# Three equal column groups in the first projection, x staged in a slab, six held-back K tiles and a norm shift on TensorE, in a hybrid encoder block

## The chip, the cores and the metric

The kernel runs on one core of a Trainium2 chip. The metric is the device time of one execution in microseconds (us). Before the change it is 1144.58 us, the median of three runs (1144.49 to 1145.9).

The engines are TensorE (PE; its loads of stationary operands are PEld), VectorE (DVE), ScalarE (ACT), GpSimd (POOL) and SyncE (SP). In this kernel SP issues nearly all loads and stores.

## The reference

One layer, 256 tokens, width 2048, float32. A combined input projection feeds eight retention heads and eight latent-attention heads; both groups are joined by an output projection. Then a norm, a feed-forward part and a second norm:

```
proj = x @ w_in                       # retention q, k, v, gate | latent c_q (768), c_kv (512), k_rope (64)
mix  = concat(retention(...), latent_attention(...)) @ w_out
x    = LN(alpha * x + mix, ln1_g, ln1_b)
h    = square(relu(x @ w_up)) @ w_down        # 2048 -> 8192 -> 2048
out  = LN(alpha * x + h, ln2_g, ln2_b)
```

with `LN(x) = (x - mean) * rsqrt(var + eps) * g + b` over the 2048 features. The 1344 latent columns of the input projection (c_q, c_kv and k_rope) and the second LN are what the change touches.

## The kernel before

**Exact products in two halves.** Each float32 operand is split into a high part, which TensorE can multiply in its faster float32r form, and a low part, the rest. ACT writes the high part (`nc.scalar.copy`, L166), DVE subtracts it from the original for the low part (L167). A product is three TensorE products: high by high, high by low, low by high. `xstat` (L264 to L277) issues them with the activations as the stationary operand and the weights moving, for each K tile, each block of 128 tokens (`tb` 0 and 1), and each group of columns. It takes a list of steps (K tiles) and, for a single bank of results, the number of that bank. `wstat` does the same with the weights stationary.

**The stream of loads.** All weights are jobs in one list, in the order of their use. A job has a load (one DMA on SP into one of `NRAW` = 3 raw buffers of 128x2048, L147 to L152) and pieces of work (`piece`, up to 1024 columns each) that split it into a high and a low tile. These tiles come from `NSLOT` = 5 slots (`wsp`); jobs with `into` are staged into other memory and take no slot. `unit()` stands between products and issues up to two further pieces, if a slot is free by the order of the program; `use(job)` issues whatever is still missing. `load_ahead` (L108) issues the loads of the job in hand and the two behind it. A load into a raw buffer waits until ACT and DVE have split what was in it. The engines run their own instructions strictly in the order in which the program issued them, so a split that waits for its load holds up what stands behind it on ACT and DVE.

**Head.** The activations x come transposed, in five loads (`x_job`, L197; after weights 0, 1, 3, 6 and 10 by `X_AFTER`). Each takes a raw buffer of the same three, and DVE splits it into `xhl`. The first weight tile is loaded in four DMAs (columns 0, 256, 512, 1024 to 1343) and split in as many steps. Meanwhile eight TensorE products on zeros (L351) are issued. Then come 16 K tiles of the latent columns (L365 to L377): for each block of tokens nine products, three parts by groups of 512, 512 and 320 columns (`MW`, L353), into six banks of PSUM. A slab `ml` of 128x8192 later holds the latent values. Slabs are three large buffers used in turn. The results are copied into it (L373) and the retention projection starts (`r` in the profile).

**Middle.** Retention, latent attention, output projection, first norm and the up product follow; the change leaves them alone.

**End.** The down product has 64 K tiles (L881), each 24 products into all eight banks (two blocks of tokens by four groups of 512 columns). The activations of four K tiles at a time are split by `r_split` (L853: ACT L857, DVE L858), issued ahead, where kt is 1, 5, 9 and so on. K tiles 60 to 63 are held back: 60 and 61 are staged in a slab (`wst2`), 62 and 63 sit in slots. They are then multiplied bank after bank (`down_bank`, L900), 12 products a bank, so that DVE can add the residual and take statistics (`residual`, L655) of one bank while TensorE works on the next. After the last bank of a block `stats` (L686) gives mean and variance, with a power on POOL (L250) for the reciprocal root. The norm is then applied in place. `finish` (L909) makes two updates on DVE and a store on SP; `finish_aside` (L918) has ACT normalise, POOL multiply by the gain and add the shift, and ACT's queue store. The first block's columns 0 to 1023 go through `finish` between the second block's banks, its columns 1024 to 2047 aside; of the second block 1536 to 2047 go aside and the rest to `finish`.

Of the kernel before, what the change touches and what calls it, by code (L numbers as in the profile page):

```python
# [33 lines left out]
NRAW = 3  # L34
NSLOT = 5
# [3 lines left out]
class Cols:  # L39
    """Columns held in pieces of 1024."""  # L40

    def __init__(self, pieces):
        self.pieces = pieces

    def __getitem__(self, key):
        i, a = divmod(key[1].start, 1024)
        return self.pieces[i][:, a:a + key[1].stop - key[1].start]


class Job:  # L50
    """One load and the pieces of work that it feeds."""

    def __init__(self, load, pieces, slotted):
        self.load = load
        self.pieces = pieces
        self.slotted = slotted
        self.emitted = 0
        self.hi = []
        self.lo = []
        self.raw = None  # L60


@with_exitstack
def kernel(
# [43 lines left out]
    def load_ahead(upto):  # L108
        while state["dma"] < min(upto, len(jobs)):
            jobs[state["dma"]].load()  # L110
            state["dma"] += 1

    def next_piece(force):
# [9 lines left out]
        load_ahead(state["job"] + NRAW)  # L123
# [4 lines left out]
    def use(job, n=None):  # L128
        while job.emitted < (len(job.pieces) if n is None else n):
            next_piece(True)  # L130
        return Cols(job.hi), Cols(job.lo)
# [10 lines left out]
    def weights(src, n, name, first=False, into=None):  # L142
        job = Job(None, [], into is None)
        cuts = [0, 256, 512, 1024, n]

        def load():
            raw = raw_tile(job, f"raw_{name}")  # L147
            if first:
                for a, b in zip(cuts, cuts[1:]):
                    nc.sync.dma_start(raw[:, a:b], src[:, a:b])  # L150
            else:
                nc.sync.dma_start(raw[:, :n], src)  # L152

        def piece(i):
            a, m = i * 1024, min(1024, n - i * 1024)
# [7 lines left out]
            for o, e in ((0, 256), (256, 512), (512, 1024)) if first and i == 0 else ((0, m),):  # L163
                c = slice(o, e)
                r = job.raw[:, a + c.start:a + c.stop]
                nc.scalar.copy(hi[:, c], r)  # L166
                nc.vector.tensor_sub(lo[:, c], r, hi[:, c].bitcast(F32))  # L167

        job.load = load
        job.pieces = [lambda i=i: piece(i) for i in range((n + 1023) // 1024)]  # L170
# [11 lines left out]
    # side streams advance one stage for each unit of the main stream of products  # L182
# [12 lines left out]
    xhl = slab.tile([P, KT, 512], F32R, tag="slab", name="xhl")  # L195

    def x_job(k0, n):  # L197
        def load(job):
            nc.sync.dma_start(raw_tile(job, f"xraw{k0}")[:, : n * S], x_t[:, k0 * S:(k0 + n) * S])

        def piece():
            v = job.raw[:, : n * S].rearrange("p (k t) -> p k t", k=n)
# [3 lines left out]
        job = other(load, [piece])  # L206

# [44 lines left out]
    def rot(dst1, dst2, raw, cs, sn, n, w):  # L252
        """Rotate n pairs of halves, all first halves ahead of all second ones; raw is used up."""
# [86 lines left out]
    for kt in range(64):  # L340
        j_down.append(weights(w_down[kt], 2048, f"wd{kt}", into=staged_down(kt - 60) if kt in (60, 61) else None))
# [689 lines left out]
```

## Time and profile before

The profile is of one execution; its times are in us from the start.

| | |
|---|---|
| runs | 1144.58 us median (1144.49, 1144.58, 1145.9) |
| profiled execution's span | 1144.0 us |
| TensorE busy | 1127.5 us |
| VectorE, ScalarE, GpSimd busy | 687.6, 506.7, 18.2 us |
| HBM read, written | 214.12 MB, 2.10 MB |
| first product of the latent columns | 4.97 |
| first product of the retention projection | 68.30 |
| first held-back product | 1109.96 |
| residual of the last bank on VectorE starts | 1131.92 |

In the rows that follow, a group of instructions is written as line, engine, operation, result<-operands, shape and count (x16). A row of the timeline or of the chain begins with its start and how long it took; several like instructions in a row are merged, and the brackets give the engine's idle time before the first of them and what ended it. A row of a table by stretches has, after the stretch, its length, the busy time of PE, PEld, DVE, ACT and POOL with counts, TensorE's granted clock (1.00 is full), the busy share of the DMA engines and GB/s. A row of DMA issues ends with the size of one and the median time from issue to landing. Products overlap in TensorE's pipeline, so what one of them costs is the distance between starts and not the duration shown for one.

### The profile page before, as it was taken

The numbers are of one execution on the slowest core, as the hardware profiler recorded it, in microseconds if no ns is written. First come the engines' busy times: TensorE is split into PE (matmuls) and PEld (weight loads), VectorE is DVE, ScalarE is ACT, GpSimd is POOL, SyncE is SP. The second block draws the span as 40 slices with busy tenths as digits, with TensorE's granted clock in tenths as the row PEclk, the third lists the DMA queues.
The fourth block names the chain that finished last, engine by engine and source line by source line (L and its number), as shares of the span: only waits on it lengthen the run. The fifth ranks groups of instructions, "written<-read, shape, count | busy, mean of one in ns | idle before, by whom it ended". The sixth has DMA issues, their size and how long they took to land.

```text
span 1144.0 us, 14163 instructions
## 1 busy us (share of the span) xinstructions
PE 1127.5 (99%) x5636; PEld 952.7 (83%) x5636; DVE 687.6 (60%) x919; ACT 506.7 (44%) x653; POOL 18.2 (2%) x23
## 2 busy tenths in 40 slices
PE   8999999999999999999999999999999999999995
PEld 7888888888888889888888888888888888888884
DVE  5776674666656786555555655555656455445567
ACT  4445664545453545444444444444434444344340
POOL 0000000000000000000000000000000000000003
PEclk9999999999999999999999999999999999999998
DMA  7765364444474625555555555555566555555561
GB/s 227 254 210 208 116 222 178 157 148 160 152 294 177 236 103 196 190 188 190 189 188 185 185 184 184 184 185 184 187 223 237 199 184 189 203 197 184 189 252 74
DMA packets 34049, 217.12 MB, mean 190 GB/s; under 512 B 4160, under 2 KB 5312, under 8 KB 10560
## 3 DMA queue, kind: packets, MB, share of 16 engines
q1 hardware_dynamic: 33552, 215.44, 53.2%
q8 instruction: 44, 0.72, 0.2%
q10 hardware_dynamic: 432, 0.79, 0.2%
q14 instruction: 21, 0.17, 0.0%
HBM read 214.12 MB, written 2.10 MB: 189 GB/s over the span
## 4 chain that ended last, share of the span: by engine, by line
PE 95%; DVE 2%; DMA 1%; POOL 1%; ACT 1%; issue 0%; SPq 0%; ACTq 0%; DVEq 0%; POOLq 0%
PE d L274 29%; PE up L584 20%; PE r L274 15%; PE up L585 10%; PE o L274 7%; PE m L274 4%; PE pu L584 2%; DMA raw_mla<-in_w_mla 1%; PE pv L274 1%; PE pu L585 1%; PE pq L274 1%; PE up L746 1%; PE pms L608 0%; PE pms L607 0%; PE up L754 0%
## 5 line engine op out<-in xcount | busy, mean ns | idle before, releaser
L584 PE MATMUL up<-x1hl,hi_wu 128*128 128x512 f32 x984 | 347.7, 399 | 0.0
L585 PE MATMUL up<-x1hl,lo_wu 128*128 128x256 f32 x984 | 276.4, 281 | 0.0
L274 PE MATMUL d<-hi_wd,rhl 128*128 128x512 f32 x992 | 248.4, 389 | 0.0
L167 DVE TENSOR_TENSOR lo_wd<-raw_wd,hi_wd 128x1024 fp32r<-128x1024 f32 x124 | 146.6, 1221 | 158.3 <-ACT hi_wd L166 158.1
L584 PEld LDWEIGHTS up<-x1hl,hi_wu 128*128 128x128 f32 x984 | 184.9, 188 | 46.0
L274 PEld LDWEIGHTS d<-hi_wd,rhl 128*128 128x128 f32 x992 | 186.2, 188 | 38.6
L166 ACT CAST hi_wd<-raw_wd 128x1024 fp32r<-128x1024 f32 x124 | 125.1, 1053 | 191.3 <-PE d L274 182.8
L167 DVE TENSOR_TENSOR lo_wu<-raw_wu,hi_wu 128x1024 fp32r<-128x1024 f32 x128 | 156.4, 1225 | 74.1 <-ACT hi_wu L166 70.0
L585 PEld LDWEIGHTS up<-x1hl,lo_wu 128*128 128x128 f32 x984 | 185.9, 189 | 0.0
L166 ACT CAST hi_wu<-raw_wu 128x1024 fp32r<-128x1024 f32 x128 | 134.1, 1051 | 83.0 <-PE up L584 80.7
L274 PE MATMUL r<-hi_ret,xhl 128*128 128x512 f32 x512 | 147.1, 397 | 0.0
L274 PE MATMUL d<-lo_wd,rhl 128*128 128x512 f32 x496 | 134.5, 389 | 0.0
L274 PEld LDWEIGHTS d<-lo_wd,rhl 128*128 128x128 f32 x496 | 93.1, 188 | 19.3
L274 PEld LDWEIGHTS r<-hi_ret,xhl 128*128 128x128 f32 x512 | 93.9, 188 | 18.3
L167 DVE TENSOR_TENSOR lo_ret<-raw_ret,hi_ret 128x1024 fp32r<-128x1024 f32 x64 | 75.7, 1220 | 23.0 <-ACT hi_ret L166 22.9
L274 PE MATMUL r<-lo_ret,xhl 128*128 128x512 f32 x256 | 79.4, 391 | 0.0
L847 ACT COPY ut<-up 128x256 f32<-128x256 f32 x64 | 23.9, 373 | 118.9 <-PE up L585 116.2
L166 ACT CAST hi_ret<-raw_ret 128x1024 fp32r<-128x1024 f32 x64 | 64.9, 1051 | 14.5 <-PE r L274 11.6
L848 DVE TENSOR_TENSOR ut<-ut,up 128x256 f32<-128x256 f32 x64 | 27.0, 421 | 65.3 <-ACT ut L847 65.3
L274 PE MATMUL o<-hi_wo,mix 128*128 128x512 f32 x208 | 57.1, 392 | 0.0
L274 PEld LDWEIGHTS r<-lo_ret,xhl 128*128 128x128 f32 x256 | 48.0, 188 | 10.4
L274 PE MATMUL m<-hi_mla,xhl 128*128 128x512 f32 (+1 forms) x192 | 46.1, 372 | 0.9 <-ACT hi_mla L166 0.8
(182 smaller groups left out, 980.7 us busy)
## 6 DMA issues: line engine op xcount, KB each, us to landing
raw_wu<-in_w_up SPq DMA_DIRECT2D x64, 1024.0 KB, 4.8
raw_wd<-in_w_down SPq DMA_DIRECT2D x64, 1024.0 KB, 4.8
raw_ret<-in_w_ret SPq DMA_DIRECT2D x32, 1024.0 KB, 4.8
raw_wo<-in_w_out SPq DMA_DIRECT2D x16, 1024.0 KB, 4.8
raw_mla<-in_w_mla SPq DMA_DIRECT2D x15, 672.0 KB, 5.5
raw_qk<-in_w_qk SPq DMA_DIRECT2D x8, 640.0 KB, 3.9
row<-in_ln_rows SPq DMA_DIRECT2D x4, 1024.0 KB, 4.8
raw_uv<-in_w_uv SPq DMA_DIRECT2D x2, 1024.0 KB, 4.7
```

What stands on the lines that cost most here:

```text
L166: nc.scalar.copy(hi[:, c], r)
L167: nc.vector.tensor_sub(lo[:, c], r, hi[:, c].bitcast(F32))
L274: nc.tensor.matmul(accs[j][:, :w], x_part, w_part[:, a:a + w], start=first and fst and i == 0, stop=last and lst and i == len(steps) - 1)
L584: nc.tensor.matmul(pb, hi[:, a:a + P], hl[:, k0 + i], start=first and i == ks[0], stop=False)
L585: nc.tensor.matmul(pb[:, 0:S], lo[:, a:a + P], hl[:, k0 + i, 0:S], start=False, stop=last and i == ks[-1])
L746: nc.tensor.matmul(pb[:, :, t], hi[:, k * P:(k + 1) * P], x1hl[:, k].rearrange("p (a t) -> p a t", a=2)[:, :, t], start=tb == 0 and k == 0 ...
L847: nc.scalar.copy(t, pb[:, S:])
L848: nc.vector.tensor_add(t, t, pb[:, 0:S])
```

## The change

1. **Columns.** The latent columns are taken in three groups of 448 (`MW`), and their weight pieces are 896 and 448 columns wide rather than 1024 and 320 (`width`).
2. **x.** The x loads go to the front of the slab `ml`, which is allocated earlier and is empty at that time, and no longer take raw buffers (`raw_user`). `load_ahead` counts raw buffers only: three weight loads ahead, and every x load that stands before the next one.
3. **First weights.** Weight tile 0 comes in three DMAs of 448 columns, the first on ACT's queue. For K tile 0 the order of the products is changed: the high weights first, by column group, for both blocks of tokens and both halves of x, then the low weights. Five products on zeros are issued ahead of it instead of eight.
4. **Held-back tiles.** `NDOWN` = 58: K tiles 58 to 63 are held back; 58 to 61 are staged in two slabs, 62 and 63 in slots. A bank has 18 products at the end.
5. **Second norm.** Nothing goes aside any more. The first block is finished by DVE between the second block's banks, and the second block's gain is multiplied in ahead of its statistics' use. For its columns 512 to 2047 the shift `b2 - mean * rstd * g2` is made by TensorE in PSUM (identity times b2, plus a diagonal of `-mean * rstd` times g2); for columns 0 to 511 DVE makes it. One update by `rstd` and the shift then ends each group of 512 columns, and all stores are on SP.

```diff
+NDOWN = 58
...
     def load_ahead(upto):
-        while state["dma"] < min(upto, len(jobs)):
-            jobs[state["dma"]].load()
+        raws = sum(j.raw_user for j in jobs[:upto]) + NRAW
+        while state["dma"] < len(jobs):
+            job = jobs[state["dma"]]
+            if job.raw_user and sum(j.raw_user for j in jobs[:state["dma"] + 1]) > raws:
+                break
+            job.load()
             state["dma"] += 1
...
-        load_ahead(state["job"] + NRAW)
+        load_ahead(state["job"])
...
         def load():
             raw = raw_tile(job, f"raw_{name}")
-            if first:
-                for a, b in zip(cuts, cuts[1:]):
-                    nc.sync.dma_start(raw[:, a:b], src[:, a:b])
-            else:
-                nc.sync.dma_start(raw[:, :n], src)
+            for i, (a, b) in enumerate(spans):
+                (nc.scalar if cuts and i == 0 else nc.sync).dma_start(raw[:, a:b], src[:, a:b])
...
+    ml = slab.tile([P, 8192], F32, tag="slab", name="ml")
+    xraw = ml[:, 0:KT * S]
...
-            nc.sync.dma_start(raw_tile(job, f"xraw{k0}")[:, : n * S], x_t[:, k0 * S:(k0 + n) * S])
+            nc.sync.dma_start(xraw[:, k0 * S:(k0 + n) * S], x_t[:, k0 * S:(k0 + n) * S])
...
-        j_mla.append(weights(w_mla[k], NMLA, f"mla{k}", first=k == 0))
+        j_mla.append(weights(w_mla[k], NMLA, f"mla{k}", width=896, cuts=(0, 448, 896, NMLA) if k == 0 else None))
...
-            if "down" not in staged:
-                staged["down"] = slab.tile([P, 8192], F32R, tag="slab", name="wst2")
-            o = (2 * i + j) * 2048
-            return staged["down"][:, o:o + 1024], staged["down"][:, o + 1024:o + 2048]
+            if (i // 2, "down") not in staged:
+                staged[i // 2, "down"] = slab.tile([P, 8192], F32R, tag="slab", name=f"wst{2 + i // 2}")
+            o = (2 * (i % 2) + j) * 2048
+            t = staged[i // 2, "down"]
+            return t[:, o:o + 1024], t[:, o + 1024:o + 2048]
...
-    for i in range(8):
+    for i in range(5):
         nc.tensor.matmul(am[1][0][:, 0:P], warm, warm, start=True, stop=True)
-    MW = (512, 512, 320)
+    MW = (448, 448, 448)
...
+        if kt == 0:
+            for fst, lst, w_part, halves in ((True, False, hi, (0, S)), (False, True, lo, (0,))):
+                for j, w in enumerate(MW):
+                    for tb in range(2):
+                        for o in halves:
+                            nc.tensor.matmul(am[tb][j][:, :w], xhl[:, 0, o + tb * P:o + (tb + 1) * P],
+                                             w_part[:, j * w:(j + 1) * w], start=fst and o == 0, stop=False)
...
-    for kt in range(60):
+    for kt in range(NDOWN):
...
-        if kt % 4 == 1:
+        if kt % 4 == 1 and kt // 4 < 15:
             r_split(kt // 4 + 1)
...
-    for kt in range(60, 64):
+    for kt in range(NDOWN, 64):
         hi, lo = use(j_down[kt])
-        w_staged.append((rhls[15], kt % 4, hi, lo, 0))
+        w_staged.append((rhls[kt // 4], kt % 4, hi, lo, 0))
...
+    def gain(j):
+        c = xt[:, 1, j * 512:(j + 1) * 512]
+        nc.vector.tensor_mul(c, c, g2[:, j * 512:(j + 1) * 512])
...
+    shift = [(acc if j < 2 else bank)(f"sh{j}") for j in range(1, 4)]
     for j in range(4):
         down_bank(1, j)
...
+        finish(0, j * 512, (j + 1) * 512)
+        residual(1, j, ad[1][j], st2[1])
+        if j < 3:
+            gain(j)
+    for j in range(1, 4):
+        nc.tensor.matmul(shift[j - 1], ident, b2[:, j * 512:(j + 1) * 512], start=True, stop=False)
     stats(1, st2[1])
...
+    gain(3)
+    nm = stat.tile([P, 1], F32, tag="lnnm", name="lnnm")
+    nc.vector.scalar_tensor_tensor(nm, mvs[1][:, 0:1], -1.0, rss[1], op0=ALU.mult, op1=ALU.mult)
+    diag, t0 = warm, xm[:, 2 * D:2 * D + 512]
+    nc.scalar.activation(diag, ident, AF.Copy, scale=nm)
+    nc.vector.scalar_tensor_tensor(t0, g2[:, 0:512], nm, b2[:, 0:512], op0=ALU.mult, op1=ALU.add)
+    for j in range(4):
+        cs = slice(j * 512, (j + 1) * 512)
+        c = xt[:, 1, cs]
+        if j:
+            nc.tensor.matmul(shift[j - 1], diag, g2[:, cs], start=False, stop=True)
+        nc.vector.scalar_tensor_tensor(c, c, rss[1], shift[j - 1] if j else t0, op0=ALU.mult, op1=ALU.add)
+        nc.sync.dma_start(out[P:2 * P, cs], c)
```

More of the change, by code (lines that the diff above doesn't have):

```diff
@@ L39, with __init__ @@
 class Cols:
-    def __init__(self, pieces):
+    def __init__(self, pieces, width):
         self.pieces = pieces
+        self.width = width
     def __getitem__(self, key):
-        i, a = divmod(key[1].start, 1024)
+        i, a = divmod(key[1].start, self.width)
         return self.pieces[i][:, a:a + key[1].stop - key[1].start]
@@ L60, in __init__ @@
         self.raw = None
+        self.width = 1024
+        self.raw_user = True
 @with_exitstack
@@ L130, in use @@
             next_piece(True)
-        return Cols(job.hi), Cols(job.lo)
+        return Cols(job.hi, job.width), Cols(job.lo, job.width)
     def free(job, pieces=None):
@@ L162, in piece @@
             job.lo.append(lo)
[L163 to L167, printed above, removed]
+            for o, e in spans if cuts else ((a, a + m),):
+                o, e = max(o, a) - a, min(e, a + m) - a
+                if o < e:
+                    r = job.raw[:, a + o:a + e]
+                    nc.scalar.copy(hi[:, o:e], r)
+                    nc.vector.tensor_sub(lo[:, o:e], r, hi[:, o:e].bitcast(F32))
         job.load = load
-        job.pieces = [lambda i=i: piece(i) for i in range((n + 1023) // 1024)]
+        job.pieces = [lambda i=i: piece(i) for i in range((n + width - 1) // width)]
         job.free = [[False] for _ in job.pieces]
@@ L195 @@
     xhl = slab.tile([P, KT, 512], F32R, tag="slab", name="xhl")
+    ml = slab.tile([P, 8192], F32, tag="slab", name="ml")
+    xraw = ml[:, 0:KT * S]
     def x_job(k0, n):
         def load(job):
-            nc.sync.dma_start(raw_tile(job, f"xraw{k0}")[:, : n * S], x_t[:, k0 * S:(k0 + n) * S])
+            nc.sync.dma_start(xraw[:, k0 * S:(k0 + n) * S], x_t[:, k0 * S:(k0 + n) * S])
         def piece():
-            v = job.raw[:, : n * S].rearrange("p (k t) -> p k t", k=n)
+            v = xraw[:, k0 * S:(k0 + n) * S].rearrange("p (k t) -> p k t", k=n)
             nc.vector.tensor_copy(xhl[:, k0:k0 + n, 0:S], v)
             nc.vector.tensor_sub(xhl[:, k0:k0 + n, S:], v, xhl[:, k0:k0 + n, 0:S].bitcast(F32))
-        job = other(load, [piece])
+        other(load, [piece]).raw_user = False
     ident = const.tile([P, P], F32, name="ident")
@@ L340 @@
     for kt in range(64):
-        j_down.append(weights(w_down[kt], 2048, f"wd{kt}", into=staged_down(kt - 60) if kt in (60, 61) else None))
+        j_down.append(weights(w_down[kt], 2048, f"wd{kt}", into=staged_down(kt - NDOWN) if NDOWN <= kt < 62 else None))
         if kt in (8, 16):
@@ L350 @@
     am = [[acc("m0"), acc("m1"), bank("m2")], [acc("m3"), acc("m4"), bank("m5")]]
-    for i in range(8):
+    for i in range(5):
         nc.tensor.matmul(am[1][0][:, 0:P], warm, warm, start=True, stop=True)
-    MW = (512, 512, 320)
-    ml = slab.tile([P, 8192], F32, tag="slab", name="ml")
+    MW = (448, 448, 448)
     qnT = ml[:, 0:2048].rearrange("p (h t) -> p h t", h=H)
@@ L367 @@
         last = kt == KT - 1
+        if kt == 0:
[5 more added lines that the diff above has]
+                                             w_part[:, j * w:(j + 1) * w], start=fst and o == 0, stop=False)
         for tb in range(2):
-            xstat(am[tb], [(xhl, kt, hi, lo, 0)], MW, kt == 0, last, tb)
+            if kt:
+                xstat(am[tb], [(xhl, kt, hi, lo, 0)], MW, False, last, tb)
             if last:
```

49 lines of the change are left out of this document (9 added, 40 removed).

## The prediction

> **What bounds the kernel now.** I read the page's busy shares and its chain first, then the chain in order of time, then the timeline of the two ends.
>
> ```profile
> PE 1127.5 (99%) x5636; PEld 952.7 (83%) x5636; DVE 687.6 (60%) x919; ACT 506.7 (44%) x653; POOL 18.2 (2%) x23
> ```
> ```profile
> 24.20 44.26 PE m L274 x213
> ...
> 435.06 0.96 PE up L754 x8
> 783.70 337.32 PE d L274 x1488
> ```
>
> PE is the bound from 24.20 on: the chain stays on it with hardly a gap up to 1121. So time can only come from PE's own work, from the head (before 24.20) and from the end (after PE's last product). The rows also give prices: 337.32/1488 = 0.2267 us for a 512-column product, 0.96/8 = 0.12 for a 256-column one. One K tile of the down product is 24 products, 5.44 us; one K tile of the latent columns (512, 512, 320) is 18.
>
> ```profile
> 0.99 3.78 PE L352 MATMUL m<-warm 128*128 128x128 f32 x16 [0.99 <-POOL warm L349]
> ...
> 2.91 0.29 DVE L203 CAST xhl<-xraw 128x256 fp32r<-128x256 f32 x1 [2.91 <-DMA xraw<-in_x_t]
> ...
> 4.97 0.64 PE L274 MATMUL m<-hi_mla,xhl 128*128 128x512 f32 x1 [0.20 <-ACT hi_mla L166]
> ...
> 9.22 1.41 ACT L166 CAST hi_mla<-raw_mla 128x1024 fp32r<-128x1024 f32 x2 [2.71 <-DMA raw_mla<-in_w_mla]
> ...
> 11.58 0.88 PE L274 MATMUL m<-lo_mla,xhl 128*128 128x512 f32 x3 [0.38 <-DVE lo_mla L167]
> ...
> 13.50 1.41 ACT L166 CAST hi_mla<-raw_mla 128x1024 fp32r<-128x1024 f32 x2 [2.87 <-DMA raw_mla<-in_w_mla]
> ...
> 15.86 0.88 PE L274 MATMUL m<-lo_mla,xhl 128*128 128x512 f32 x3 [0.32 <-DVE lo_mla L167]
> ...
> 21.83 1.41 ACT L166 CAST hi_mla<-raw_mla 128x1024 fp32r<-128x1024 f32 x2 [4.56 <-DMA raw_mla<-in_w_mla]
> ...
> 24.20 0.87 PE L274 MATMUL m<-lo_mla,xhl 128*128 128x512 f32 x3 [0.38 <-DVE lo_mla L167]
> ...
> 68.30 0.63 PE L274 MATMUL r<-hi_ret,xhl 128*128 128x512 f32 x2
> ```
>
> In the head PE waits three times for the low half of a K tile (1, 2 and 4, at 11.58, 15.86, 24.20), each time 2.4 us after its load landed and ACT began on it. These loads were issued late: the x loads took raw buffers that weights wanted. From 24.20 five groups of three and eleven K tiles of six groups remain: (68.30 - 24.20)/(5 + 66) = 0.62 us a group, 3.72 a K tile.
>
> **Head, part by part.** *Groups of 448.* No 448-column product is in the trace. On the line through the two uniform streams it costs 0.2267 - 64 x (0.2267 - 0.12)/256 = 0.200 us, so a K tile 3.60; the mixed groups of three cost 0.62 where the same line gives 0.60. Bounds: 0.62 kept (nothing gained) and 0.60 (0.12 per K tile). I take 0.60, the nearest uniform rows.
>
> *x in its own slab.* The x loads no longer wait for raw buffers; tiles 1 and 2 are issued at the start, so DMA is not left without work. What is late next is DMA's own rate.
>
> ```profile
> 5.28:24.20 18.92, 17.08 (x76) 12.64 (x75) 10.84 (x17) 7.32 (x11) 0.00 (x0) 1.00 0.79 258
> 24.20:68.46 44.26, 44.26 (x214) 37.56 (x215) 29.41 (x43) 21.63 (x32) 0.00 (x0) 1.00 0.76 245
> ```
> ```profile
> L166 ACT CAST hi_mla<-raw_mla 128x1024 fp32r<-128x1024 f32 x5 | 5.2, 1049 | 11.3 <-DMA raw_mla<-in_w_mla 10.4 <-DVE lo_mla L167 1.0
> L166 ACT CAST hi_mla<-raw_mla 128x512 fp32r<-128x512 f32 x1 | 0.6, 617 | 0.6 <-DMA raw_mla<-in_w_mla 0.6
> ...
> L167 DVE TENSOR_TENSOR lo_mla<-raw_mla,hi_mla 128x1024 fp32r<-128x1024 f32 x4 | 4.9, 1226 | 7.2 <-ACT hi_mla L166 7.2
> ...
> L167 DVE TENSOR_TENSOR lo_mla<-raw_mla,hi_mla 128x512 fp32r<-128x512 f32 x1 | 0.7, 692 | 0.8 <-ACT hi_mla L166 0.8
> ```
>
> Between these sizes a 896-column piece takes 0.94 on ACT and 1.09 on DVE, so a tile's low half is ready 2.13 us after landing (2.4 before). The first load (128 KB of x) is in at 2.9; at 258 GB/s tile 0's 688 KB follow by 5.6 and tile 1 with its x (819 KB) by 8.7 (9.2 before). Low half 10.9, and 15 products later, at 13.9, K tile 1 is done. Tile 2 (950 KB more) lands at 12.4, low half 14.5, just when PE wants it; K tile 2 ends at 17.5. Tile 4 (1900 KB more, x included) lands at 19.8, low half 21.9, wanted at 21.7. From there 3.0 + 11 x 3.60 ends the stage at 64.5 instead of 68.30. That is **3.8 us less**, which I take. At 245 GB/s all landings slip and it is 3.2. Bounds 1.9 (groups stay at 0.62 as well) and 4.5 (no wait after K tile 1, tile 1 in at 8.2).
>
> *First weights by piece, and the reordered K tile 0.* Three loads of 224 KB, the first on ACT's queue ahead of its table load: first product about 4.4 instead of 4.97, K tile 0 done near 8.5. K tile 1's high half is there only at 8.7 + 0.94 = 9.7, so this buys nothing: that wait hides it, and K tile 0 may slip by 1.2 before it costs. *Five warm-up products for eight* end near 3.35 (3.78/16 = 0.24 an instruction, two a call) and leave PE idle to 4.4. Warm-up ran at half the pace of later f32 products (0.43 for two instructions of 256 columns, below). Bounds: nothing, and 1.7 us if all of K tile 0 ran at half pace (0.39 for 18 products, ending 11.4); I take nothing, since the slack of 1.2 covers half pace up to 7.5.
>
> **Held-back tiles.** Banks now take 18 products each, 4.08 us, and start two K tiles earlier. PE's work is the same; the question is whether the data is there.
>
> ```profile
> 1087.95 2.01 ACT L166 CAST hi_wd<-raw_wd 128x1024 fp32r<-128x1024 f32 x2 [3.43 <-PE d L274]
> ...
> 1100.74 1.05 ACT L857 CAST rhl<-rr 128x1024 fp32r<-128x1024 f32 x1
> ...
> 1109.45 2.00 ACT L166 CAST hi_wd<-raw_wd 128x1024 fp32r<-128x1024 f32 x2 [1.42 <-DMA raw_wd<-in_w_down]
> ```
> ```profile
> 1089.04 2.36 DVE L167 TENSOR_TENSOR lo_wd<-raw_wd,hi_wd 128x1024 fp32r<-128x1024 f32 x2 [3.08 <-ACT hi_wd L166]
> ```
> ```profile
> 1109.96 1.52 PE L274 MATMUL d<-wst,rhl 128*128 128x512 f32 x6
> ```
> ```profile
> 1090.29 0.33 SPq L152 DMA_DIRECT2D raw_wd<-in_w_down  x1
> ```
> ```profile
> raw_wd<-in_w_down SPq DMA_DIRECT2D x64, 1024.0 KB, 4.8
> ```
> ```profile
> raw_wu<-in_w_up SPq DMA_DIRECT2D x2, 1024.0 KB, 5.2
> ```
>
> Before, tile 63 landed at 1109.4, just ahead of the first held-back product at 1109.96. Now that product comes at 1109.96 - 10.88 = 1099.08 (clock of before). The casts at 1087.95 are tiles 57 (second piece) and 58 (first); from there staged tiles wait for no slot, only for loads and order. A load waits until DVE has split the tile three back. DVE's two pieces at 1089.04 end at 1091.4, and each further piece adds 1.14, so tile 60's load is issued at 1090.29 as now, 61's at 1092.6, 62's at 1094.9. A lone load takes 4.8 us, and the two up-weight loads of the second row, issued within 2.5 us of each other, took 5.2, so 60 lands at 1095.1 and 62 at 1100.2. Tile 60's casts and splits take 3.5 more, to 1098.6; only then is 63 issued, landing at 1103.4. On ACT the split of the last activations (L857) is now queued behind tile 62's first piece, and so behind its load: two casts after 1100.2 it ends at 1102.3. K tile 60 needs it six products after 1099.08, at 1100.44: **1.9 us** of stall. DVE's half of it follows tile 62's, at 1103.7, so the third product of that K tile waits **1.0** more and K tiles 61 and 62 end at 1105.3. Behind it DVE still has 62's second and 63's first piece, to 1106.0, where PE wants 63's low half at 1105.6: **0.4**. Sum **+3.3**; the other seven banks find all data. Bounds 0 (all in time) and about 6 (rival D).
>
> **The end.** The first block's norm goes wholly to DVE: per bank two updates at 0.75, residual and statistics 1.38, gain 0.69, in all 3.6 of the 4.08 us; PE hides it. ACT and POOL lose the aside work; SP takes over ACT's three stores, one a bank, with nothing queued behind them.
>
> ```profile
> 1124.37 0.75 DVE L913 SCALAR_TENSOR_TENSOR xm<-xm,lnmv,row 128x512 f32<-128x512 f32 x1
> ...
> 1131.92 0.69 DVE L658 SCALAR_TENSOR_TENSOR xm<-xm,d 128x512 f32<-128x512 f32 x1 [0.81 <-PE d L274]
> ...
> 1133.90 0.54 POOL L250 TENSOR_TENSOR lnrs<-rs,mhalf 128x1 f32<-128x1 f32 x1 [1.61 <-DVE rs L249]
> ```
> ```profile
> 170.05 0.60 PE L607 MATMUL pms<-ml 128*128 128x256 f32 x2
> 170.48 0.59 PE L608 MATMUL pms<-ml 128*128 128x256 f32 x2
> ```
> ```profile
> 420.57 0.94 POOL lnrs L250
> ```
> ```profile
> 1140.52 0.83 SPq L916 DMA_DIRECT2D out<-xm  x2
> ```
> ```profile
> out<-xm SPq DMA_DIRECT2D x4, 256.0 KB, 2.2
> ...
> out<-xm SPq DMA_DIRECT2D x2, 128.0 KB, 1.9
> ```
>
> Count from the residual at 1131.92 as 0. Now the last store is issued at 1140.9, the second of the two at 1140.52, and with the 1.9 us of its half size lands at about 11.0. After: the power on POOL starts at 1.98 and takes 0.54, or 0.94 as at 420.57, where DVE was running beside it as `gain(3)` will; I take 0.94. Then nm at 3.1, ACT's diagonal 3.5 (an estimate, under the 0.62 of its 512-column cast), and three f32 products of 512 columns at 0.86 (0.43 for 256). DVE's four updates follow them: 4.6, 5.3, 6.2, 7.0; the last store lands at 9.25. **-1.8** (bounds -2.2, the power at 0.54, and -1.4, another 0.4 for waits between engines that no row shows). The three products that add b2 take 2.6 us beside DVE's chain.
>
> The Trainium skill ("SBUF — State Buffer", "SBUF: two separate sides") says that GpSimd and a VectorE operation with two SBUF inputs lock a shared port for a whole instruction. By that the power would wait out `gain(3)`, 0.6 rather than 0.4, and the end be 0.2 later; the trace's 0.94 agrees with the direction.
>
> **Sum.** -3.8 + 3.3 - 1.8 = -2.3 against the profiled 1144.0; that lies 0.58 under the median, so 1144.58 - 2.3, about **1142.2**. Forecast, chance 0.62, own range 1141.0 to 1143.6.
>
> **Rivals.** *B, the held-back tiles are in time* (0.13): no stall, -5.6, 1139.0. For it: ACT is busy 44% of the span and DVE 60%. Against: three loads behind each other need 8 us, and tile 63 had 0.5 us to spare before.
>
> *C, 448-column products gain nothing* (0.12): head 1.9 less, 1144.1. For it: the mixed stream's unexplained 0.02 in 0.62. Against: both uniform streams lie on one line.
>
> *D, slower* (0.07): the three loads drag as they do at 54.5.
>
> ```profile
> raw_ret<-in_w_ret SPq DMA_DIRECT2D x3, 1024.0 KB, 7.4
> ```
> ```profile
> 1131.72:1135.10 3.38, 0.17 (x1) 0.00 (x0) 2.42 (x6) 0.42 (x1) 1.12 (x2) 1.00 0.21 78
> 1135.10:1138.51 3.41, 0.00 (x0) 0.00 (x0) 3.41 (x4) 0.39 (x1) 2.86 (x2) 0.50 0.01 3
> ```
>
> With 7.4 us a load, 62 lands at 1102.3 and PE idles from 1100.44 to 1104.4, which is over the 3.38 us after which its clock halved at the end; 63 lands at 1106. Stall 6, and 3.4 us at half clock cost 1.7: -5.6 + 7.7 = +2.1, 1146.7. It decides from a landing of 62 after 1101.8. Against it: steady down loads take 4.8. The Trainium skill ("TensorE: Matmul & The Clock Gate", Part 1) has the same rule, one idle window of about 3.4 us.
>
> *E, the change doesn't do what it says in the head* (0.06): DMA lands the tiles no sooner with a full queue than with gaps. Tile 4's low half then comes at 21.83 + 2.13 = 24.0, the stage ends at 66.6, 1.7 gained: 1144.4.
>
> **How the numbers follow.** A measurement of this kernel tells about 0.2%, 2.3 us, from no change: faster is below 1142.3, slower above 1146.9. The forecast lies on that line: 0.37 of its 0.62 below. Faster 0.37 + B = 0.50; same 0.45 with C, E and most of D; slower 0.05. The range 1139.8 to 1145.2 takes in C, E and the forecast with B's near side, and leaves out the rest of B and D.
>
> **What would show it.** A latent K tile at 3.60, stage end near 64.4; PE idle before K tile 60 for L857's successor, some 1.9 us; last store landing 9.2 after the last residual's start. No idle in the first bank would make B true; K tiles at 3.72, C; a halved clock near the first bank, D.

## The result and the profile after

The changed kernel takes 1147.63 us (median of 21 executions, 1144.79 to 1149.33) against 1145.01 us of the kernel before, timed beside it (21 executions). The ratio is 1.0018, with a 95% interval of 1.0012 to 1.0025: a small loss, where 2.4 us of gain had been forecast. Two executions are set aside in the ratios as disturbed, one of e1 below at 2296.57 us and one of the kernel before, timed beside e9 to e12, at 1244.21 us. The profiled execution took 1149.33 us, the longest of the 21, with a span of 1147.5, which is 3.5 us over the profiled span before (1144.0). So what follows explains the worst execution; how it bears on the median comes after it. Three numbers make up these 3.5 us.

| | before | after | difference |
|---|---|---|---|
| first product of the retention projection | 68.30 | 65.86 | -2.44 |
| residual of the last bank starts | 1131.92 | 1137.09 | +5.17, and seen from the earlier start +7.61 |
| from there to the end of the span | 12.10 | 10.45 | -1.65 |

The head and the end gain 4.1 us together; what lies between them loses 7.6. The waits of TensorE at the end of the kernel show where (line waited for, then us in total, number, longest; the change puts `xstat` on L286 and `r_split` on L876 and L877):

```profile
PE d L286 <- ACT rhl L876: 3.5, 1, 3.5
PE sh L959 <- ACT warm L953: 1.0, 1, 1.0
PE d L286 <- DVE rhl L877: 0.7, 1, 0.7
```

Both waits of the down product are for the split of the last activations (`rhl`), and both lie in the first held-back bank. This is its timeline on TensorE, and below it ScalarE's in the same time:

```profile
1096.63 1.52 PE L286 MATMUL d<-wst,rhl 128*128 128x512 f32 x6
1101.61 0.73 PE L286 MATMUL d<-wst,rhl 128*128 128x512 f32 x2 [3.46 <-ACT rhl L876]
1103.06 2.07 PE L286 MATMUL d<-wst,rhl 128*128 128x512 f32 x4 [0.72 <-DVE rhl L877]
1104.93 0.63 PE L286 MATMUL d<-hi_wd,rhl 128*128 128x512 f32 x1
1105.36 0.63 PE L286 MATMUL d<-lo_wd,rhl 128*128 128x512 f32 x1
...
1107.49 3.72 PE L286 MATMUL d<-wst,rhl 128*128 128x512 f32 x12
```
```profile
1092.90 2.00 ACT L175 CAST wst<-raw_wd 128x1024 fp32r<-128x1024 f32 x2 [2.55 <-DMA raw_wd<-in_w_down]
1096.79 2.00 ACT L175 CAST wst<-raw_wd 128x1024 fp32r<-128x1024 f32 x2 [1.89 <-DMA raw_wd<-in_w_down]
1099.57 1.04 ACT L175 CAST hi_wd<-raw_wd 128x1024 fp32r<-128x1024 f32 x1 [0.78 <-DMA raw_wd<-in_w_down]
1100.52 1.04 ACT L876 CAST rhl<-rr 128x1024 fp32r<-128x1024 f32 x1
```

Read ScalarE's rows from the bottom. The split of the activations starts at 1100.52 because ScalarE first waits for tile 62's load, which came at 1099.5. That load was issued at 1092.38 and took 7.09 us; the usual down load takes 4.8. The three loads 60 to 62 were issued only 2.27 us apart, each before the one ahead of it had landed. That alone doesn't make 7.09: in the traces of e2, e3 and e4 below, with the same spacing, loads 61 and 62 took 4.9 to 5.4 us, and in e8 7.2 and 7.4 again. What made them longer in some executions was not found.

The rest of the loss is in the distance between products. After the wait they follow each other at 0.43 us (1104.93, 1105.36), not 0.23. The table by stretches says why (length, then busy time of PE, PEld, DVE, ACT, POOL with counts, the granted clock, DMA share, GB/s):

```profile
1095.60:1099.01 3.41, 2.55 (x12) 1.78 (x10) 1.89 (x2) 2.00 (x2) 0.00 (x0) 1.00 0.97 377
1099.01:1102.43 3.42, 0.73 (x2) 0.30 (x2) 3.01 (x4) 2.86 (x4) 0.00 (x0) 1.00 0.85 309
1102.43:1105.84 3.41, 2.78 (x7) 2.20 (x8) 3.41 (x4) 1.97 (x3) 0.00 (x0) 0.50 0.64 245
1105.84:1109.25 3.41, 3.41 (x10) 2.64 (x9) 1.96 (x3) 0.00 (x0) 0.00 (x0) 0.50 0.64 267
1109.25:1112.66 3.41, 3.41 (x17) 2.82 (x16) 0.05 (x1) 0.00 (x0) 0.00 (x0) 1.00 0.00 0
```

The clock was halved from 1102.43 to 1109.25. TensorE waited 4.2 us, and half of the 6.2 us in which it then worked at half clock is another 3.1: together 7.3 of the 7.6.

The mean granted clock is on record for each of the 21 executions. Two such stretches lower it to 0.997, and one to 0.9985. Six executions have 0.996 or 0.997, the profiled one among them; they took 1147.69 to 1149.33 us. Three have 1.000, which leaves no room for such a stretch, and took 1144.79, 1145.17 and 1146.86. In the other twelve (0.998 and 0.999) there was at most one, or only a part of one at the very end. So the median execution loses less to the clock than the 3.1 us of the profiled one.

In the head, the products of K tile 0 (L384) and the first of K tile 1, ScalarE's high half of tile 1, and the end of the stage:

```profile
5.07 4.85 PE L384 MATMUL m<-hi_mla,xhl 128*128 128x448 f32 x12 [1.58 <-ACT hi_mla L175]
9.72 1.58 PE L384 MATMUL m<-lo_mla,xhl 128*128 128x448 f32 x6
11.14 0.77 PE L286 MATMUL m<-hi_mla,xhl 128*128 128x448 f32 x3
...
65.86 0.63 PE L286 MATMUL r<-hi_ret,xhl 128*128 128x512 f32 x2
```
```profile
9.20 1.41 ACT L175 CAST hi_mla<-raw_mla 128x896 fp32r<-128x896 f32 x2 [3.03 <-DMA raw_mla<-in_w_mla]
```

The first twelve products take (9.72 - 5.07)/12 = 0.39 us each, nearly twice the 0.20 of later ones: TensorE stood idle for 1.58 us after its five warm-up products and K tile 0 runs at half pace until about 10 us. Tile 1's first high half is there at 9.20 + 0.95 = 10.15; TensorE comes for it only at 11.14.

The end, from the last residual on:

```profile
1137.09 0.69 DVE L677 SCALAR_TENSOR_TENSOR xm<-xm,d 128x512 f32<-128x512 f32 x1 [0.49 <-PE d L286]
...
1139.13 0.86 POOL L262 TENSOR_TENSOR lnrs<-rs,mhalf 128x1 f32<-128x1 f32 x1 [15.40 <-DVE rs L261]
1140.02 0.16 DVE L951 SCALAR_TENSOR_TENSOR lnnm<-lnmv,lnrs 128x1 f32<-128x1 f32 x1 [0.43 <-POOL lnrs L262]
1140.22 0.40 ACT L953 ACTIVATE warm<-ident,lnnm 128x128 f32<-128x128 f32 x1 [35.82 <-DVE lnnm L951]
...
1140.67 2.84 PE L959 MATMUL sh<-row,warm 128*128 128x512 f32 x6 [1.05 <-ACT warm L953]
...
1141.84 2.46 DVE L960 SCALAR_TENSOR_TENSOR xm<-xm,lnrs,sh 128x512 f32<-128x512 f32 x3
```

The chain residual, power, `nm`, diagonal, products, updates runs without a gap worth naming; the last store is issued at 1144.33 and lands 2.2 us later, 9.46 after the residual's start.

### The profile page after: what moved, and what is told of

Same layout as the page of the kernel before. It is cut to its first block, busy times and chain, and to the rows that moved or that the text cites. A ratio compares the mean times of both kernels' runs of the same rounds, so it can differ in the third digit from the quotient of the medians.

```text
span 1147.5 us, 14159 instructions
## 1 busy us (share of the span) xinstructions
PE 1134.4 (99%) x5642; PEld 961.2 (84%) x5642; DVE 690.2 (60%) x922; ACT 504.4 (44%) x650; POOL 9.7 (1%) x17
## 4 chain that ended last, share of the span: by engine, by line
PE 96%; DVE 1%; DMA 1%; ACT 1%; issue 0%; POOL 0%; POOLq 0%; ACTq 0%
PE d L286 29%; PE up L603 20%; PE r L286 15%; PE up L604 10%; PE o L286 7%; PE m L286 5%; PE pu L603 2%; PE pv L286 1%; PE pu L604 1%; PE pq L286 1%; DMA raw_wd<-in_w_down 1%; PE up L765 1%; PE m L384 1%; PE pms L627 0%; PE pms L626 0%; DVE wst L176 0%
## 5 line engine op out<-in xcount | busy, mean ns | idle before, releaser
L286 PE MATMUL d<-hi_wd,rhl 128*128 128x512 f32 x960 | 241.4, 390 | 0.0
L176 DVE TENSOR_TENSOR lo_wd<-raw_wd,hi_wd 128x1024 fp32r<-128x1024 f32 x120 | 141.9, 1222 | 151.1 <-ACT hi_wd L175 150.9
L286 PEld LDWEIGHTS d<-hi_wd,rhl 128*128 128x128 f32 x960 | 180.7, 188 | 37.7
L175 ACT CAST hi_wd<-raw_wd 128x1024 fp32r<-128x1024 f32 x120 | 121.1, 1054 | 182.4 <-PE d L286 175.9
L286 PE MATMUL r<-hi_ret,xhl 128*128 128x512 f32 x512 | 147.1, 397 | 0.0
L286 PE MATMUL d<-lo_wd,rhl 128*128 128x512 f32 x480 | 130.7, 390 | 0.0
L286 PEld LDWEIGHTS r<-hi_ret,xhl 128*128 128x128 f32 x512 | 93.9, 188 | 18.2
L286 PEld LDWEIGHTS d<-lo_wd,rhl 128*128 128x128 f32 x480 | 90.4, 188 | 18.8
L286 PE MATMUL r<-lo_ret,xhl 128*128 128x512 f32 x256 | 79.4, 391 | 0.0
L286 PE MATMUL o<-hi_wo,mix 128*128 128x512 f32 x208 | 57.1, 392 | 0.0
L286 PEld LDWEIGHTS r<-lo_ret,xhl 128*128 128x128 f32 x256 | 48.0, 188 | 10.4
L286 PEld LDWEIGHTS o<-hi_wo,mix 128*128 128x128 f32 x208 | 38.7, 188 | 7.9
```

Source lines behind the costliest of these rows:

```text
L175: nc.scalar.copy(hi[:, o:e], r)
L176: nc.vector.tensor_sub(lo[:, o:e], r, hi[:, o:e].bitcast(F32))
L286: nc.tensor.matmul(accs[j][:, :w], x_part, w_part[:, a:a + w], start=first and fst and i == 0, stop=last and lst and i == len(steps) - 1)
```

## The experiments

The theory was: the head and the end work, and the loss is made in the first held-back bank, by the stall and by the halved clock that follows it. The rivals were a loss in the new end, one spread over the whole kernel, and, inside the bank, the order on ScalarE against the lateness of the loads. Each kernel was timed in five rounds beside the kernel before. The runs e1 to e4, e5 to e8 and e9 to e12 were timed on three chips, so across these groups the ratios are safer to compare than the times. Where two intervals overlap widely, the difference of the medians is not clear of the scatter.

| | executions | us (median) | ratio to before, 95% interval |
|---|---|---|---|
| as changed | 21 | 1147.63 | 1.0018 [1.0012, 1.0025] |
| e4: only six held back | 5 | 1150.16 | 1.0042 [1.0030, 1.0054] |
| e1: as changed, four held back | 10 | 1148.29 | 1.0027 [1.0017, 1.0036] |
| e2: as changed, split of activations ahead | 11 | 1146.65 | 1.0010 [1.0002, 1.0019] |
| e5: as changed, staged tiles loaded sooner | 11 | 1143.57 | 0.9985 [0.9976, 0.9993] |
| e8: as changed, 4 products of zeros in the idle time | 11 | 1148.00 | 1.0020 [1.0011, 1.0029] |
| e10: as changed, 12 products of zeros | 11 | 1146.66 | 1.0014 [1.0005, 1.0023] |
| e3: as changed, eight warm-ups | 11 | 1146.82 | 1.0014 [1.0005, 1.0022] |
| e7: head alone | 11 | 1143.53 | 0.9987 [0.9979, 0.9996] |
| e12: head alone, eight warm-ups | 11 | 1143.70 | 0.9991 [0.9982, 1.0000] |
| e11: 448-column groups alone | 11 | 1144.69 | 0.9997 [0.9988, 1.0006] |
| e6: e5 with eight warm-ups | 11 | 1142.75 | 0.9978 [0.9969, 0.9987] |
| e9: e6 with the split ahead | 6 | 1140.90 | 0.9971 [0.9960, 0.9983] |

### Six held-back tiles alone (e4)

The kernel before with part 4 of the change and nothing else.

```diff
-    for kt in range(60):
+    for kt in range(NDOWN):    # 58
...
-    for kt in range(60, 64):
+    for kt in range(NDOWN, 64):
```

> The kernel before with only the held-back tiles made six. The prediction's step gave +3.3 us for it (stall 1.9, 1.0 and 0.4): 1148. Theory of now (stall of 4 us and a halved clock for some 7 us in the first bank): +5 to +8 us, 1150 to 1153. Rival (the stall is a matter of the other parts of the change, which shift the loads): within 1.5 us of the kernel before.

It cost 4.9 us (1150.16 against 1145.22). The profiled execution waited 1.8 us for ScalarE's split and 0.7 for VectorE's, 2.5 in all, and the clock halved none the less:

```profile
1100.96:1104.37 3.41, 1.60 (x6) 1.02 (x7) 3.28 (x3) 3.41 (x5) 0.00 (x0) 1.00 1.00 423
1104.37:1107.78 3.41, 3.41 (x10) 2.63 (x9) 2.78 (x4) 0.56 (x1) 0.00 (x0) 0.50 0.77 293
```

So the loss belongs to the held-back tiles themselves, not to the rest of the change, and the longest wait before a halved clock was 1.8 us, about half of what the prediction thought necessary. The loads 61 and 62 took 5.0 and 5.4 us here, close to what the prediction took, and the waits are below its 3.3; the clock is what it had left out. All five executions have a mean clock of 0.993 or 0.994, where the kernel before nearly always has 0.996 or 0.997.

### Four held-back tiles with the new end (e1)

```diff
-NDOWN = 58
+NDOWN = 60
```

> Only four K tiles are held back again (NDOWN 60); head and tail stay as changed. Theory (the six held-back tiles stall the first bank and let the clock halve, some 7.6 us of span in the profiled run): no PE wait of over 0.5 us in the first bank and no half clock there. Against that a bank of the second block is 2.6 us of products beside about 3.5 us of VectorE work, so the last residual comes up to 2.5 us late. Net 3 to 7 us under the changed kernel, 1141 to 1144.5 us. Rival (the loss lies in the tail or is spread over the body): the time stays within 1.5 us of the changed kernel, 1146 to 1149.

The stall went, as expected, but the time did not: 1148.29, which lies where the rival had put it. The rival was still wrong about the changed kernel, since the loss here is a new one that this run's own edit makes in the end. Against the head alone (e7, 1143.53), which has the same four tiles and the old end, the new end costs 4.8 us here. Its stretches behind the last bank, and its diagonal products:

```profile
1132.37:1135.78 3.41, 0.00 (x0) 0.00 (x0) 3.06 (x7) 0.00 (x0) 0.67 (x1) 1.00 0.20 77
1135.79:1139.20 3.41, 2.55 (x3) 1.18 (x4) 2.10 (x4) 0.40 (x1) 0.18 (x1) 0.50 0.18 68
```
```profile
1136.65 5.49 PE L959 MATMUL sh<-row,warm 128*128 128x512 f32 x6 [4.32 <-ACT warm L953]
```

A bank is 2.7 us of products here, and VectorE needs 3.5 for it (residuals at 1122.57, 1126.08, 1129.58, 1133.08). TensorE is done early, stands idle for 4.32 us, and meets the diagonal at half clock: three products take 5.49 us, not 2.84, and every update and store behind them is late. The expectation had priced VectorE's lag (up to 2.5) but not this. The two parts of the change belong together: the new end needs banks of six tiles, which take TensorE longer (4.08 us) than VectorE (3.5).

### The split ahead of tile 60 (e2)

```diff
         def into(j):
+            r_split(15 if (i, j) == (2, 0) else 16)    # 16 does nothing
...
-        if kt % 4 == 1 and kt // 4 < 15:
+        if kt % 4 == 1 and kt // 4 < 14:
```

> Six tiles stay held back; the split of the last four activation tiles is put on ScalarE and VectorE ahead of K tile 60's split instead of behind the first half of tile 62's. No load is moved. Theory A (the stall is that order): the products of K tile 60 follow those of 59 without a wait, K tile 63's low half is late by about 1.1 us, no half clock, and the last d product comes 6 us sooner: 1141 to 1142.5 us. Theory B (the loads 60 to 63 themselves come too late, whatever the order): PE still waits over 3 us before the products of K tile 62 or 63, the clock still halves, 1145 us or more.

By its time this is theory B: 1146.65, a median 1.0 us under the changed kernel, though the two scatter over each other (1144.38 to 1148.28 here). The wait for `rhl` is gone, and in its place there are waits for the weights behind it, 2.3 us in all and not over 3:

```profile
PE d L286 <- DVE lo_wd L176: 1.2, 2, 0.8
PE d L286 <- ACT hi_wd L175: 1.1, 1, 1.1
```
```profile
1101.97:1105.38 3.41, 1.51 (x4) 0.76 (x5) 2.73 (x4) 1.99 (x2) 0.00 (x0) 1.00 1.01 406
1105.38:1108.79 3.41, 3.41 (x9) 2.66 (x9) 2.15 (x3) 0.00 (x0) 0.00 (x0) 0.50 0.50 207
```

TensorE eats a held-back tile in 0.68 us; the loads land 2.5 us apart or more. Whatever stands first on ScalarE, tile 62's low half and tile 63 are late. Tile 63's load took 4.68 us, no longer than usual, but was issued only at 1097.97, so its lateness comes from the late issue and not from a slow transfer. In this execution three short waits, 2.3 us in all, halve the clock again. It is the slowest of the eleven: six of them have a mean clock of 1.000 and took 1144.38 to 1146.65, the other five (0.997 to 0.999) 1146.88 to 1148.28. So theory B was right about the loads, and about the clock only for a part of the executions.

### The staged tiles loaded sooner (e5), with eight warm-ups (e6), and with the split ahead (e9)

The jobs of tiles 58 to 61 are moved in the list of loads to behind 44, 47, 50 and 53; the order of the products stays. e6 adds three warm-ups; e9 adds to that the split of the last activations at K tile 55.

```diff
-    for kt in range(64):
-        j_down.append(weights(w_down[kt], 2048, f"wd{kt}", into=...))
+    for kt in [q for k in (*range(58), 62, 63) for q in ((k, 58 + (k - 44) // 3) if k in (44, 47, 50, 53) else (k,))]:
+        j_down[kt] = (weights(w_down[kt], 2048, f"wd{kt}", into=...))
...
-    for i in range(5):    # e6, e9
+    for i in range(8):
...
             if tb == 1:
+                r_split(15 if kt == 55 else 16)    # e9 alone
```

> Six tiles held back, five warm-ups, but the four staged tiles are loaded and split between the tiles 44 to 54, where the transfers have room, instead of one behind the other at the end; only tiles 62 and 63 come last. Theory (the whole loss is the stall and the halved clock of the first bank, because the loads of the held-back tiles start only 2.3 us apart at the end): no PE wait of over 0.3 us there, full clock, span near 1139.9 and a time of 1141 to 1142, which is faster than both kernels. Rival (something else in the held-back banks costs the time, such as VectorE or the ScalarE order): still a stall of over 1.5 us and a time above 1144.

> The run before this one with eight warm-up products in place of five. Theory: both causes are apart, so it takes another 0.7 us off (first r product near 65.5 instead of 66.2): 1140 to 1141.5. Rival (the head's gain is lost again further on): same as with five.

> Staged tiles sooner, eight warm-ups, and the split of the last four activation tiles put on ScalarE ahead of tile 57's second half instead of behind tile 63's pieces. In the run without this last edit PE still waited 0.3 and 0.7 us for that split, 1.4 us from the first to the last late product. Theory: these go, no wait is left in the first bank, 1.4 us faster: 1141 to 1141.8. Rival (the split only changes places with a weight piece that is then as late): 1142.3 to 1143.

e5 took 4.1 us off the changed kernel (1147.63 to 1143.57), less than hoped, because the split of the activations was still 0.3 and 0.7 us late, now behind tile 63's pieces. The time lies between what the theory and the rival had given. The clock stayed full. e6 gave another 0.8, the size that was expected, though from a higher start. e9 took these last waits away and made 1140.90 us, 1.8 under e6, where 1.4 had been expected. Of its six executions five took 1140.52 to 1141.78, less than any of e6; the sixth, which was not traced, took 1144.77 at a mean clock of 0.998, so a halved clock still comes at times. By the ratio it is 0.29% under the kernel before, and it beats both kernels. Its first bank:

```profile
1095.70 2.88 PE L286 MATMUL d<-wst,rhl 128*128 128x512 f32 x12
1098.42 0.39 PE L286 MATMUL d<-hi_wd,rhl 128*128 128x512 f32 x1
```
```profile
1095.67:1099.08 3.41, 3.41 (x16) 2.82 (x15) 1.23 (x1) 0.83 (x1) 0.00 (x0) 1.00 0.14 58
```

Twelve products without a wait, TensorE busy for the whole stretch, and almost nothing left for DMA to bring (0.14). The same six tiles and the same work on them: apart from three more warm-up products at the start, only the place of four loads and one split in the program is different from the changed kernel.

### Filling the idle time (e8, e10)

Products of zeros, added into the first bank between K tiles 59 and 60, leave its sums as they are. They test the clock by itself: no wait is taken away, TensorE only gets more to do.

```diff
+        if tb == j == 0:
+            xstat(ad[0], w_staged[:2], (512,) * 4, False, False, 0, banks=(0,))
+            for i in range(4):    # e10: 12
+                nc.tensor.matmul(ad[0][0][:, 0:P], warm, warm, start=False, stop=False)
```

> The changed kernel with four f32 products of 128 columns with zeros, 1.7 us in all, put between the held-back K tiles 59 and 60 of the first bank, where PE stands idle. Theory (the clock halves because the share of a 3.4 us stretch in which PE works falls under about a half): the idle time is filled, no half clock in the first bank, and with more work on the PE path the kernel is 1.5 to 3.4 us faster than as changed, 1144.3 to 1146. Rival (the clock follows the wait itself, or something else): half clock stays, and the time is 0 to 1.7 us longer than as changed, 1147.5 to 1149.3.

> As the filled run before it, with twelve products of zeros in place of four. Four filled only 0.85 us at full clock (0.21 us each), and the profiled stretch of 3.4 us still had PE at work for only 0.22 of it. Theory of the clock (the share of work in the stretch decides): twelve give 2.6 us, the share rises over 0.6, no half clock in the first bank, and the time falls under that of the changed kernel by 1 to 2.5 us: 1145 to 1146.6. Rival (the wait itself decides): half clock stays, 1147.5 to 1150.

With four, the time and the clock came out as the rival had said, but the test had not been made: four were too few to raise the share of work. They were sized by the warm-up's pace, which is half pace; at full clock four take 0.85 us, not 1.7, and in the profiled execution the loads were late enough to leave TensorE at work for 0.74 of 3.41 us:

```profile
1097.73:1101.14 3.41, 0.74 (x7) 0.55 (x5) 3.09 (x3) 2.84 (x4) 0.00 (x0) 1.00 0.67 276
1101.15:1104.56 3.41, 2.95 (x6) 1.95 (x7) 3.41 (x4) 3.02 (x4) 0.00 (x0) 0.50 0.84 308
```

Twelve raised it. The clock stays full, and with 2.8 us of useless work on its critical engine (1099.00 to 1101.78) the kernel's median is 1.0 us below that of the changed kernel. The times of the two overlap (1145.44 to 1147.38 against 1144.79 to 1149.33); the clock does not leave it open: nine of the eleven executions have a mean clock of 1.000 and two 0.999, against three of 21 with 1.000 as changed.

```profile
1100.67:1104.08 3.41, 2.70 (x17) 2.00 (x16) 3.27 (x3) 3.32 (x5) 0.00 (x0) 1.00 0.91 380
1104.08:1107.49 3.41, 3.25 (x15) 2.33 (x14) 3.38 (x5) 0.68 (x1) 0.00 (x0) 1.00 0.67 231
```

So the halved clock is a cost of its own beside the stall, and filling the idle time with work keeps it away; that it goes by the share of work in a stretch is set out under the last heading.

### The head (e3, e7, e11, e12)

e3 is the changed kernel with eight warm-ups. e7 is the change with `NDOWN` = 60 and the end of before; e12 is e7 with eight warm-ups; e11 is the kernel before with only `MW`, the widths of the pieces and of tile 0's loads changed.

```diff
-    for i in range(5):    # e3, e12
+    for i in range(8):
...
-    MW = (512, 512, 320)    # e11
+    MW = (448, 448, 448)
```

> Eight warm-up products in place of five, all else as changed. Theory (K tile 0 runs at half clock because PE idles 1.7 us between the last warm-up and the first product): full clock is granted near 5.3 us, products of K tile 0 are 0.2 us apart instead of 0.37, K tile 1 starts when its hi half is there, near 10.2 instead of 11.1, and the latent stage ends 0.9 us sooner: 0.9 us under the changed kernel. Rival (the clock comes at a fixed distance from the first K tile, or K tile 1's data come later too): stage end unchanged within 0.2 us.

> Only the head of the change (448-column groups, staged x, first weights by piece, five warm-ups); four tiles held back and the old end. The prediction's step gave 3.8 us less than the kernel before, 1141.4. Theory of now: 2 to 2.5 us less, 1142.7 to 1143.3, with K tile 0 at half clock until about 10 us and a K tile at 3.65 us, or 3.72 where the products keep the slower spacing of 0.207.

> The kernel before with nothing but the three groups of 448 columns (pieces of 896 and 448, first tile in three pieces, all on SyncE's queue, eight warm-ups, x through the raw buffers as before). The prediction's 0.200 us per product would give 0.12 us for each of ten K tiles that wait for nothing, 1.2 us, and 1144. Theory of now: 0.07 us each where the products keep 0.203 us, nothing where they keep 0.207: 0 to 1 us less than before, and the rest of the head's gain belongs to x.

> The head of the change alone with eight warm-ups in place of five (four tiles held back, old end). With five it was 1.7 us under the kernel before. Theory: K tile 0 runs at full clock from about 6 us on instead of 8 to 10, K tile 1 then waits for its data at about 10.0, another 0.5 to 0.8 us: 1142.4 to 1143.1. Rival (K tile 1's data set its start in both): 1143.5 as with five.

The head alone gains 1.7 us (e7), less than either figure. The groups alone gain nothing that can be told by the median (e11, 0.3 us), but its executions lie apart, four at 1143.21 to 1143.70 and seven at 1144.33 to 1145.52. In the traced one, 1143.70, the retention projection starts at 65.98, 2.3 us sooner than before, although x still goes through the raw buffers. How the gain of the head is shared between the groups and x is therefore open. Eight warm-ups lower the median by 0.8 in e3 (1147.63 to 1146.82, within the scatter) and in e6 (clear of it, beside e5 on one chip), and not in e12. There seven executions took 1142.39 to 1143.84 at a mean clock of 0.996 and four 1144.87 to 1146.39 at 0.994 or 0.995, as one more stretch at half clock would make it; with that e12 does not decide. The traces do show the mechanism. With eight warm-ups (e9) the first twelve products of K tile 0 take 0.28 us each, the next six 0.20, and K tile 1 starts 1.5 us sooner than as changed:

```profile
5.06 3.50 PE L384 MATMUL m<-hi_mla,xhl 128*128 128x448 f32 x12 [0.29 <-ACT hi_mla L175]
8.40 1.38 PE L384 MATMUL m<-lo_mla,xhl 128*128 128x448 f32 x6
9.62 0.79 PE L286 MATMUL m<-hi_mla,xhl 128*128 128x448 f32 x3
10.60 1.01 PE L286 MATMUL m<-lo_mla,xhl 128*128 128x448 f32 x3 [0.19 <-DVE lo_mla L176]
```

Some 0.6 us of this is given back at once: the low half of tile 1 and its second piece are then what is late, and the stage ends 0.9 us sooner (64.95 against 65.86). This pair is the most favourable one. In all traces with the head of the change, K tile 1 starts at 10.20 to 11.14 with five warm-ups and at 9.62 to 10.04 with eight. Where the products keep 0.203 us, the stage ends at 65.62 on average with five (five traces, 65.07 to 66.20) and at 65.32 with eight (four traces, 64.95 to 65.51): 0.3 us, less than the medians of e3 and e6 show.

## Why the prediction was wrong, step by step

**What bounds the kernel.** Right: TensorE, the head and the end, and nothing between them moved. One remark was off: the span of the profiled execution is not 0.58 us from its time. Each timed execution here is 1.7 to 2.1 us longer than its span, so that one belongs to the 1145.9 us, above the median. The differences were subtracted from the median, so the forecast did not change by it.

**The terms, by the runs that hold one each.** The held-back tiles alone cost 4.9 (e4) where +3.3 was put; the head alone gains 1.7 (e7) where 3.8 was put; the end gains 1.65 in the trace where 1.8 was put. These add up to +1.5, and +2.6 was measured (+2.1 by the ratio). So both of the first two terms failed, and 0.5 to 1 us is not accounted for by single parts.

**Groups of 448: mis-sized.** 0.200 us a product was taken from a line through two sizes. Measured are 0.203, a K tile of 3.65, and in two of the twelve profiled executions that have these groups (e2, e10) 0.207, a K tile of 3.72, as with 512, 512 and 320. Fourteen K tiles make that 0.7 or 1.7 us. Rival C was right about the products in these two.

**x in its own slab: right in what it does.** Tile 1 landed at 9.18, forecast 8.7, tile 2 at 11.48, forecast 12.4 (the 258 GB/s that the forecast reckoned with are of a stretch in which DMA was busy for only 0.79), and from K tile 1 on TensorE had no wait. What it is worth is not shown by itself (see e11).

**Five warm-ups, costed at nothing: the step that failed in the head.** The cover named was K tile 1's wait, with 1.2 us of slack that "covers half pace up to 7.5". Half pace lasted to about 10. With the first product at 5.07 in place of 4.4 (the first piece of the weights and the first x were issued together, and x took 3.5 us to land instead of 2.15), K tile 0 ended a microsecond after tile 1 was ready. K tile 1 was done at 14.78, forecast 13.9. This 0.9 and 0.5 from the pace of the later products make up the 1.4 by which the profiled execution's head, -2.44, fell short of -3.8. By e7 the head is worth -1.7.

**Held-back tiles: right place, and the step that failed.** The split behind tile 62's piece, the waits for its ACT and then its DVE half, and tile 62 as the late load were all as forecast. The stall was 4.2 us against 3.3 in the profiled execution, where loads 61 and 62 took 6.7 and 7.1 us and 5.2 had been taken. In the traces of e3 and e4, where these loads took 4.9 to 5.4, the stall was 2.3 and 2.5, less than forecast. What the sum of +3.3 left out is the clock, which it put at nothing: 3.1 us more in the profiled execution (two stretches), half of 3.41, or 1.7, in e3 and e4 (one stretch). That was in rival D, at a chance of 0.07, with 7.7 for stall and clock (7.3 in the profiled execution) and 1146.7 in all (1147.63). That these come so close is luck: its 7.7 was 6.0 of stall and 1.7 of clock, measured were 4.2 and 3.1, and that in the slowest execution; its total also counted on the full gain of the head. Its landing condition was just met (tile 62 at 1099.47, which is 1101.9 on the clock of before, against 1101.8). Its condition for the clock was too strict: it asked for over 3.38 us of unbroken idle time, as the Trainium skill ("TensorE: Matmul & The Clock Gate", Part 1) does with one idle window of about 3.4 us. Here waits of 1.8 and 0.7 (e4), and three short ones of together 2.3 (the traced execution of e2), were enough; the measurement decides.

**Rival B** (the tiles are in time) needed what e9 does. There the forecast for B, 1139.0, is missed by 1.9. The head's shortfall by e7, 2.1, would be enough to explain that; but e9 has eight warm-ups and e7 five, so this is an estimate.

**The end: right.** -1.8 forecast, -1.65 measured. The power took 0.86 (0.94; 0.54 before, where VectorE had nothing beside it), the diagonal came 3.13 after the residual's start (3.5), the last store landed at 9.46 (9.25). Not seen was its condition: with four tiles held back it would have cost 4.8.

**Rival E** (the loads come no sooner) is out: tile 2 landed at 11.48, before at 13.48, and K tile 1 and all later ones had their data.

## What to carry to other kernels

Work that is held back to the end is used up faster than it can be loaded (0.68 us a tile in the first bank, against 2.5 or more between landings), so its loads have to be issued where the transfers have room and not last in the list; and a step that other work needs should not stand on an in-order engine behind a piece that waits for a load. After any stall on TensorE, look at its busy time in stretches of 3.4 us: where that falls under half, the stall costs about half of the next stretch too. Work without use in the idle time kept the clock full here; whether the time gained by it is more than scatter is not settled (e10). A gain from TensorE in a last step holds only while the steps ahead keep TensorE busy.

## What was not expected of the hardware

**The clock goes by shares of fixed stretches.** In all traces each stretch of half clock between two of full clock lasts 3.41 us or twice that. Cut along these borders, a stretch with TensorE busy for 0.73, 1.51 or 1.60 of 3.41 us was followed by half clock, and one with 1.74 was not. That one is in the end of e9:

```profile
1133.22:1136.64 3.42, 1.74 (x5) 0.44 (x3) 2.25 (x3) 0.00 (x0) 0.00 (x0) 1.00 0.63 232
1136.64:1138.98 2.34, 0.00 (x0) 0.00 (x0) 0.00 (x0) 0.00 (x0) 0.00 (x0) 1.00 0.29 109
```

The border is near one half. The way back is stricter: at half clock, 2.55 busy out of 3.41 (e1), 2.78 (as changed) and 2.95 (e8) were followed by half clock again, 2.94 (e1) and 3.41 by full. So its border lies near 2.9, and these two readings do not fix it more closely. The borders lie at a different distance from the kernel's start in each execution, so the same stall may be cut in two or fall into one stretch. That fits the wide scatter of the changed kernel (4.5 us, mean clocks from 0.996 to 1.000) beside e6 (0.7 us, 1142.36 to 1143.06, 0.999 or 1.000), but only one execution of each was traced.

**One stream of products, two paces.** The 448-column products keep 0.203 us in ten of the twelve traced executions and 0.207 in two, from K tile 3 to the end of the stage, with the same instructions. As changed, and e2, eighteen products (28.77 to 32.42, and 28.88 to 32.60):

```profile
28.77 1.38 PE L286 MATMUL m<-hi_mla,xhl 128*128 128x448 f32 x6
...
32.42 0.97 PE L286 MATMUL m<-hi_mla,xhl 128*128 128x448 f32 x4
```
```profile
28.88 1.40 PE L286 MATMUL m<-hi_mla,xhl 128*128 128x448 f32 x6
...
32.60 0.78 PE L286 MATMUL m<-hi_mla,xhl 128*128 128x448 f32 x3
```

3.65 and 3.72 us for the same K tile. What sets the pace was not found. The two clusters of e11, which have the same mean clock, may come from it; those of e12 go with the clock.
